# Seven half-size products for eight in w_down, for sixteen of 22 gated tiles

## The chip, the cores and the metric

One Trainium2 chip, one of its cores. The metric is the device time of one execution in microseconds (us); lower is better. In the profile PE is TensorE (matrix products), PEld its weight loads, DVE VectorE, ACT ScalarE, POOL GpSimd, SP SyncE, which issues the transfers.

## The reference

One step of a decoder layer for 1024 prompt tokens and 8 sample tokens that share the weights. The tail of the layer is what matters here:

```python
x = x + concat(ya, yb) @ w_out
x = x + cross_attn(rmsnorm(x, g_attn), mk, mv, w_q, w_o)
h = rmsnorm(x, g_ffn)
x = x + (silu(h @ w_gate) * (h @ w_up)) @ w_down     # D_MODEL 1024, D_FF 2816
y = rmsnorm(x, g_final)
```

All is float32.

## The kernel before

**Layout.** Activations lie transposed: channels on the 128 partitions, tokens along the free dimension. There are T = 1032 tokens: even prompt positions, odd ones, then the samples. The hidden dimension of 2816 is 22 tiles of 128 channels (`FF_TILES`). TH = 516 is half the tokens, TQ = 258 a quarter.

**Precision.** A float32 product is made of three passes (`PASSES`): each operand is split into a high part of TensorE's reduced type and the low rest; high x high, high x low and low x high are summed in PSUM. `split` makes the two parts: the high one on ACT or Pool, the low one (a subtraction of two SBUF operands) on DVE or Pool.

**The gated tiles.** For gate and value of a tile f the kernel already uses seven half-size products for eight (a 2 x 2 scheme of Strassen's kind): w_gate and w_up of the tile are the two column halves of one matrix, the model dimension is halved, and the tokens are halved. The operands on the token side are seven blocks `A11 ... S4`, made once and held for the whole stage in 14 of the 19 big buffers (tag `op`); those on the weight side are made tile by tile in `sums_prep` (two buffers of sums, `Ta` and `Tb`). `product` issues one of the seven: 4 blocks of channels x 3 passes x 2 quarters of 258 columns, 24 matmuls, into one two-bank PSUM buffer (two products of three) or a pair of one-bank buffers (the third). `plus` adds a product from PSUM onto a quarter of `su[f]` on DVE, `first_two`'s first product is copied by ACT, `gated` and `times_value` form silu(gate) x value on DVE, Pool and ACT. The result of tile f, 128 x 1032, goes out to the array `hd` in HBM.

**w_down.** After the 22 tiles, `down(c)` takes the hidden tiles in four chunks of four: `hidden(c)` loads each from `hd` and splits it; for each of the eight output tiles of 128 channels, 4 tiles x 3 passes x 3 thirds of 344 columns (`step3`), 36 matmuls (the profile's dn, L447), then one addition of 1032 columns onto the residual `x2` on DVE (L1409). A weight block `w_dn` of 128 x 1024 serves two output tiles: four hidden tiles by 256 outputs. The last six hidden tiles are handled by `last_down` (fd, L1435) in three spans of tokens, with the final RMSNorm of one span beside the products of the next.

**What sets the order.** Every operation is a task with costs, reads and writes (`Program.add`). `Program.order` lays the tasks out on the engines by a greedy plan: at each step the task that can start first, with a priority by program order for ties. A task with both `DVE` and `Pool` in its costs goes to whichever would end it sooner; tasks marked `lock` on DVE and all tasks on Pool are planned to exclude each other. `later` lowers the priority of preparations, and buffers come by tag from a fixed `capacity`:

```python
capacity = {"op": 19, "raw": 3, "w": 2, "scr": 3, "acc": 1, "R": 1, "sm": 4, "sst": 2, "rows": 2, "mm": 2, "ms": 2}
```

`mm` and `ms` are PSUM (three banks and one bank each). The plan is fixed when the program is built: each engine runs its tasks in that order and waits on semaphores.

Of the kernel before, what the change touches and what calls it, by code (L numbers as in the profile page):

```python
# [8 lines left out]
F32 = mybir.dt.float32  # L9
# [230 lines left out]
def hybrid_step_kernel(ctx: ExitStack, tc: tile.TileContext, io):  # L240
# [126 lines left out]

    chunks = [(0, 4), (4, 4), (8, 4), (12, 4), (16, 6)]
    last_blocks = [("w_dn", 16), ("w_dn2", 0), ("w_dn", 17), ("w_dn", 18), ("w_dn2", 1), ("w_dn", 19)]
# [12 lines left out]
    upto = len(seq)  # L382
    seq += [("w_dn", j) for j in range(16)] + last_blocks

# [875 lines left out]

    def product(w, col, b, steps=1):
# [12 lines left out]
        def emit(e, js):  # L1274
            for j in js:
                cols = slice(col + j * P, col + (j + 1) * P)
                for p, (wi, xi) in enumerate(PASSES):
                    for c in range(2):
                        e.matmul(bank(c), w[:, wi, cols], block(b, j, xi)[:, c * TQ : (c + 1) * TQ],  # L1279
                                 start=j == 0 and p == 0, stop=j == 3 and p == 2)  # L1280
# [10 lines left out]

    su = {}

# [4 lines left out]
    def plus(f, q, q2, sums):  # L1298

        a, o = part(f, q), part(f, q2)  # L1300
        from_sums(sums, "DVE", dve, lambda e, src, sl: e.tensor_tensor(as_banks(o(sl), src), src, as_banks(a(sl), src), ALU.add),  # L1301
                  [(su[f], q)], [(su[f], q2)])

# [5 lines left out]
    def gated(f, q):  # L1309
# [4 lines left out]
        times(f, q, R, RF)  # L1314

    def times_value(f, q):
        times(f, q, part(f, 2 + q), [(su[f], 2 + q)])

    def first_two(f, between=lambda: None):
        G = gu_w[f][0]  # L1320
        su[f] = op_buf(f"su{f}", (P, 4, TH))
        o = part(f, 1)
        from_sums(product(G, 0, A11, 4 if f < AHEAD else 1), "ACT", lambda n: act(n, True),
                  lambda e, src, sl: e.activation(as_banks(o(sl), src), src, AF.Copy), [], [(su[f], 1)])
        between()
        plus(f, 1, 0, product(G, 512, A12, 4 if f < AHEAD else 1))
        gated(f, 0)

    def sixth(f):
        plus(f, 1, 2, product(gu_w[f][2], 0, S2, 4 if not f else 1))  # L1330

    def others(f):
        _, U, Ta, Tb = gu_w[f]
        plus(f, 2, 3, product(Ta, 512, S3))
        fifth = product(Tb, 0, S1)
        plus(f, 2, 2, fifth)
        plus(f, 3, 1, product(Tb, 512, A22))
        plus(f, 3, 3, fifth)
        gated(f, 1)
        times_value(f, 1)  # L1340
        plus(f, 2, 2, product(U, 0, S4))
        times_value(f, 0)
        dma(lambda: hd[f], lambda: su[f][:, 0:2].rearrange("p h n -> p (h n)"), 4 * P * T, r=[(su[f], 0), (su[f], 1)], w=[("hd", f)])

    def later(work, bias="prep"):
        pg.later = BIAS[bias]
        work()
        pg.later = 0

    for n in O_ORDER:  # L1350
# [28 lines left out]

    x2 = [op_buf(f"x2_{j}") for j in range(4)]  # L1380
    hops = {c: [] for c in range(5)}

    def x2k(n):
        return [(x2[n // 2], n % 2, c) for c in range(len(LAST_SPANS))]

    state["upto"] = len(seq)
    for _ in range(2):
        w_load()

    def hidden(c):  # L1390
        for f in range(chunks[c][0], sum(chunks[c])):
            t = scr(f"ht{f}")
            dma(lambda t=t: t[:], lambda f=f: hd[f], 4 * P * T, r=[("hd", f)], w=[(t,)])
            ho = op_r(f"ho{f}")
            split(lambda p, ho=ho: ho[:, p], lambda p, ho=ho: (ho, p), lambda t=t: t[:], T, [(t,)])
            hops[c].append(ho)

    def down(c):
        for n in range(KT):
            j, i = n // 2, n % 2  # L1400
# [8 lines left out]
            add({"DVE": dve(T)}, lambda e, j=j, i=i, ps=ps: e.tensor_tensor(  # L1409
                ch3(x2[j][:, i]), ps[:, :, :CW], ch3(x2[j][:, i]), ALU.add), all3(ps) + x2k(n), x2k(n))  # L1410

    hidden(0)
    for c in range(4):
        later(lambda: hidden(c + 1))
        down(c)

# [5 lines left out]
    def last_down(c, n):  # L1422
# [8 lines left out]
        def emit(e, ks):  # L1431
            for k in ks:
                w, col = (wa, k * 256 + (n % 2) * P) if k < 4 else (wb, (k - 4) * 512 + (n % 4) * P)
                for p, (wi, xi) in enumerate(PASSES):
                    e.matmul(view(), w[:, wi, col : col + P], hops[4][k][:, xi, sl],  # L1435
                             start=(k == 0 and p == 0), stop=(k == 5 and p == 2))

        for w, keys, ks in ((wa, ka, range(4)), (wb, kb, (4, 5))):
            add({"PE": 0.000425 * 3 * len(ks) * width}, lambda e, ks=ks: emit(e, ks),
                keys + [(hops[4][k], p) for k in ks for p in range(2)], [(ps,)])  # L1440
        j, i = n // 2, n % 2
        xk = (x2[j], i, c)
        add({"DVE": dve(width)}, lambda e: e.tensor_tensor(x2[j][:, i, sl], view(), x2[j][:, i, sl], ALU.add), [(ps,), xk], [xk])
        if n < KT - 1 or c < len(LAST_SPANS) - 1:
# [139 lines left out]
```

## Time and profile before

| | us |
|---|---|
| median of 3 runs | 1268.94 (1266.14 to 1269.2) |
| the profiled execution | 1269.62, its span 1267.6 |
| granted TensorE clock, mean | 0.993 |
| gate and value products (pr), from 587.4 | 418.5 |
| w_down, tiles 0 to 15 (dn), from 1005.9 | 181.4 |
| w_down, tiles 16 to 21 (fd), from 1187.3 to the last product | 69.4 |

The times of the stages come from the chain of work that ended last, which the prediction shows with the other lines that it uses. A row of a group reads: line, engine, operation, output<-inputs by the program's names, shape, count; then busy time, mean ns of one; then the idle time of the engine just before them and what ended it. A row of the chain or the timeline starts with start and length in us. The page cuts the span into 40 slices and gives each a digit, the busy share in tenths:

```
PE   8999997999999999999999999999999999999996
DVE  7899888667367786579776766767666754312445
POOL 3578741032101102214141314232333622122100
```

PE is full from slice 18 on. The w_down stage is slices 32 to 37, where DVE's digits are lowest.

### The profile page before, as it was taken

What the parts mean: (1) busy time and instruction counts of PE and PEld (TensorE: products, weight loads), DVE (VectorE), ACT (ScalarE), POOL (GpSimd) and SP (SyncE); (2) the same over time, 40 slices, a digit from 0 to 9 for tenths busy, and PEclk for the clock granted to TensorE, in tenths of its full rate; (3) what the DMA queues carried; (4) which work ended last, traced back from release to release, by engine and by line L of the source; (5) the groups of instructions that cost most, each with busy time, mean ns of one, the idle gap of its engine ahead of it and who ended that gap; (6) DMA issues with size and microseconds to landing.
All of it is one profiled execution on the core that took longest, in us unless ns stands there. A gap on an engine that the chain in (4) does not pass through costs nothing.

```text
span 1267.6 us, 20915 instructions
## 1 busy us (share of the span) xinstructions
PE 1232.6 (97%) x8620; PEld 1212.6 (96%) x8620; DVE 844.3 (67%) x1369; ACT 476.8 (38%) x655; POOL 365.8 (29%) x304
## 2 busy tenths in 40 slices
PE   8999997999999999999999999999999999999996
PEld 7999976999999889999999999999999999999996
DVE  7899888667367786579776766767666754312445
ACT  6766648454233444453322222222222322201343
POOL 3578741032101102214141314232333622122100
PEclk9999997999999999999999999999999999999999
DMA  7447686644265673232212222121213853111112
GB/s 277 103 86 164 147 236 176 205 103 158 91 219 198 232 258 144 84 117 68 84 68 93 75 84 84 67 84 68 101 68 132 325 189 107 50 51 50 51 51 84
DMA packets 48431, 159.49 MB, mean 126 GB/s; under 512 B 7184, under 2 KB 11984, under 8 KB 47056
## 3 DMA queue, kind: packets, MB, share of 16 engines
q1 hardware_dynamic: 44736, 145.06, 32.7%
q0 software_dynamic: 3600, 13.11, 6.0%
q8 instruction: 67, 1.10, 0.4%
q14 instruction: 28, 0.23, 0.1%
HBM read 130.85 MB, written 27.30 MB: 125 GB/s over the span
## 4 chain that ended last, share of the span: by engine, by line
PE 78%; DVE 7%; issue 6%; DMA 4%; ACT 2%; POOL 2%; SPq 0%; DVEq 0%; POOLq 0%; ACTq 0%
PE pr L1279 33%; PE dn L447 14%; PE ps L447 12%; PE fd L1435 5%; PE oa L447 4%; PE ob L447 4%; DVE cacc L653 2%; DMA raw<-in_w_v 2%; PE pv L1048 2%; PE sc L990 2%; POOL w L351 1%; PE psg L447 1%; PE psv L447 1%; DMA xa<-x1d 1%; DMA w<-in_w_in 1%
## 5 line engine op out<-in xcount | busy, mean ns | idle before, releaser
L447 PE MATMUL dn<-ho,w 128*128 128x344 f32 x1152 | 181.6, 320 | 0.0
L447 PEld LDWEIGHTS dn<-ho,w 128*128 128x128 f32 x1152 | 181.4, 188 | 0.0
L1301 DVE TENSOR_TENSOR su<-pr,su 128x258 f32<-128x258 f32 (+1 forms) x204 | 108.8, 557 | 85.7 <-PE pr L1279 85.1
L1279 PE MATMUL pr<-ab,wTa 128*128 128x258 f32 x1056 | 134.2, 283 | 0.8 <-DVE su L1301 0.8
L1279 PE MATMUL pr<-ab,wG 128*128 128x258 f32 x1056 | 133.9, 283 | 0.8 <-ACT wU L340 0.8
L340 ACT ACTIVATE w<-raw 128x1024 fp32r<-128x1024 f32 (+2 forms) x54 | 52.8, 979 | 215.0 <-PE dn L447 107.6
L1279 PEld LDWEIGHTS pr<-ab,wTa 128*128 128x128 f32 x1056 | 130.1, 189 | 1.0 <-issue 1.0
L1279 PEld LDWEIGHTS pr<-ab,wG 128*128 128x128 f32 x1056 | 129.8, 189 | 1.1 <-ACT wU L340 1.1
L1279 PE MATMUL pr<-ab,wTb 128*128 128x258 f32 x1056 | 130.6, 283 | 0.0
L1279 PEld LDWEIGHTS pr<-ab,wTb 128*128 128x128 f32 x1056 | 128.6, 190 | 0.0
L351 POOL TENSOR_TENSOR w<-raw,w 128x1024 fp32r<-128x1024 f32 (+1 forms) x30 | 68.9, 2297 | 203.6 <-ACT w L340 199.3
L447 PE MATMUL ps<-xop,w 128*128 128x344 f32 x720 | 114.1, 320 | 0.7 <-DMA w<-in_w_in 0.7
L447 PEld LDWEIGHTS ps<-xop,w 128*128 128x128 f32 x720 | 113.3, 188 | 0.9 <-DMA w<-in_w_in 0.9
L1409 DVE TENSOR_TENSOR x<-dn,x 128x1032 f32<-128x1032 f32 x32 | 39.4, 1231 | 98.2 <-PE dn L447 98.2
L447 PE MATMUL ps<-xq,w 128*128 128x344 f32 x576 | 94.8, 321 | 0.0
L447 PE MATMUL po<-oo,w 128*128 128x344 f32 x576 | 91.0, 320 | 0.4 <-DVE oo L1053 0.4
L447 PEld LDWEIGHTS po<-oo,w 128*128 128x128 f32 x576 | 90.7, 188 | 0.7 <-DVE oo L1053 0.7
L447 PEld LDWEIGHTS ps<-xq,w 128*128 128x128 f32 x576 | 90.6, 188 | 0.1
L653 DVE SCALAR_TENSOR_TENSOR cacc<-glu,vec,cacc 128x511 f32<-128x511 f32 (+14 forms) x116 | 77.0, 740 | 0.0
L1435 PE MATMUL fd<-ho,w 128*128 128x388 f32 (+1 forms) x432 | 69.2, 321 | 0.0
L1435 PEld LDWEIGHTS fd<-ho,w 128*128 128x128 f32 x432 | 68.4, 188 | 0.5
L1306 DVE TENSOR_TENSOR su<-su,Rf 128x516 f32<-128x516 f32 x67 | 55.6, 832 | 18.1 <-ACT su L1313 17.4
(281 smaller groups left out, 1973.0 us busy)
## 6 DMA issues: line engine op xcount, KB each, us to landing
gr<-in_w_gu SPq DMA_DIRECT2D x44, 512.0 KB, 3.3
hd<-su SPq DMA_DIRECT2D x22, 516.0 KB, 2.9
ht<-hd SPq DMA_DIRECT2D x22, 516.0 KB, 6.2
raw<-in_w_dn SPq DMA_DIRECT2D x22, 512.0 KB, 3.3
spcache_k<-in_cache_k SPq DMA_DIRECT2D x12, 512.0 KB, 4.8
raw<-in_w_in SPq DMA_DIRECT2D x10, 512.0 KB, 5.4
w<-in_w_in POOLq DMA_DIRECT2D x9, 512.0 KB, 6.5
x<-in_xT SPq DMA_DIRECT2D x8, 516.0 KB, 6.3
```

The lines of the kernel that those rows point to most:

```text
L340: e.activation(dst(0), src(), AF.Copy, scale=1.0 if gain is None else gain)
L351: e.tensor_tensor(dst(1), src(), f32(dst(0)), ALU.subtract)
L447: e.matmul(ps[:, c, :CW], w[:, wi, cols], x[:, xi, c * CW : (c + 1) * CW], start=first and p == 0, stop=last and p == 2)
L653: e.scalar_tensor_tensor(acc[h][:, n:], src[:, : HALF - n], w, acc[h][:, n:], ALU.mult, ALU.add)
L990: e.matmul(bank()[:, i * NMEM : (i + 1) * NMEM], qop[2 * h + dt][:, qi, tt * P : (tt + 1) * P], kk[:, ki, 2 * (h % 2) + dt], start=(dt == ...
L1048: e.matmul(ps[:, c], v[:, vi, m, col : col + P], pT[h][m][:, pi, sl], start=(m == 0 and p == 0), stop=(m == 1 and p == 2))
L1279: e.matmul(bank(c), w[:, wi, cols], block(b, j, xi)[:, c * TQ : (c + 1) * TQ], start=j == 0 and p == 0, stop=j == 3 and p == 2)
L1301: from_sums(sums, "DVE", dve, lambda e, src, sl: e.tensor_tensor(as_banks(o(sl), src), src, as_banks(a(sl), src), ALU.add), [(su[f], q)], ...
L1306: add({"Pool": pool_tt(TH), "DVE": dve(TH)}, lambda e: e.tensor_tensor(o(), o(), b(), ALU.mult), r + [(su[f], q)], [(su[f], q)], lock=True)
L1409: add({"DVE": dve(T)}, lambda e, j=j, i=i, ps=ps: e.tensor_tensor(ch3(x2[j][:, i]), ps[:, :, :CW], ch3(x2[j][:, i]), ALU.add), all3(ps) + ...
L1435: e.matmul(view(), w[:, wi, col : col + P], hops[4][k][:, xi, sl], start=(k == 0 and p == 0), stop=(k == 5 and p == 2))
```

## The change

The first sixteen hidden tiles go through w_down by the same seven-for-eight scheme. A chunk of four tiles is two halves of two tiles (the inner dimension), the tokens are two halves, and 256 outputs are two halves of 128; `down(u)` does one weight block: seven products of 2 blocks x 3 passes x 2 quarters, 12 matmuls each, 16 blocks in all.

- **Token side.** The seven operand blocks of a chunk are formed where the tiles are made: of a pair of tiles (f even, then f odd) the even one's result is kept in the scratch buffer `he`, and four additions or subtractions of 516 columns (`combine`, DVE or Pool) make the sums. Blocks go out to the array `hb` in HBM in three transfers a pair (one, two and four quarters of tiles) instead of two to `hd`. `down_blocks` loads a block of 128 x 1032 and splits it: seven a chunk instead of four hidden tiles.
- **Weight side.** `dn_prep` makes four sums of 256 columns for each weight block (DVE or Pool) and splits 512, 1024 and 256 columns instead of 1024.
- **Output side.** `into` adds each product from PSUM onto a quarter on DVE, the first product of a block onto two; quarters 4 and 5 (`pp`) and quarter 3 of `x2` gather partial results, started in the first chunk by copies on ACT. In the last chunk six additions of 516 for each block (`both`, `combine`) make the outputs out of them.
- **Order.** Preparations for block u + 1 and the next chunk's blocks are added ahead of `down(u)` with lowered priority; the hidden tiles 16 to 18 are loaded ahead of the last block, 19 to 21 after it. The numbering of the seven blocks is changed so that those written together lie together.

The last six tiles, `last_down` and the final norm stay.

```diff
-A11, A12, A22, S1, S2, S3, S4 = range(7)
+A12, A22, S4, S1, A11, S2, S3 = range(7)
 O_ORDER = (0, 4, 1, 5, 2, 6, 3, 7)
 AHEAD = 2
+CHUNKS, FIRST_LAST = 4, 16
+DOWN_ORDER = (A11, S2, A12, S3, S1, A22, S4)
...
-    hd = dram.tile([FF_TILES, P, T], F32, name="hd")
+    hd = dram.tile([FF_TILES - FIRST_LAST, P, T], F32, name="hd")
+    hb = dram.tile([CHUNKS, 7, P, 2, TH], F32, name="hb")
...
+    def product(w, cols, xs, steps=1):
+        nj = len(xs[1])
         i = state["products"]
         state["products"] += 1
         if i % 3 < 2:
...
         def emit(e, js):
             for j in js:
-                cols = slice(col + j * P, col + (j + 1) * P)
                 for p, (wi, xi) in enumerate(PASSES):
                     for c in range(2):
-                        e.matmul(bank(c), w[:, wi, cols], block(b, j, xi)[:, c * TQ : (c + 1) * TQ],
-                                 start=j == 0 and p == 0, stop=j == 3 and p == 2)
-        for n in range(0, 4, 4 // steps):
-            js = range(n, n + 4 // steps)
+                        e.matmul(bank(c), w[:, wi, cols(j)], xs[0](j, xi)[:, c * TQ : (c + 1) * TQ],
+                                 start=j == 0 and p == 0, stop=j == nj - 1 and p == 2)
+        for n in range(0, nj, nj // steps):
+            js = range(n, n + nj // steps)
             add({"PE": 0.1195 * 6 * len(js)}, lambda e, js=js: emit(e, js),
-                [(w, 0), (w, 1)] + [bkey(b, j, p) for j in js for p in range(2)], [k for _, _, k in sums])
+                [(w, 0), (w, 1)] + [k for j in js for k in xs[1][j]], [k for _, _, k in sums])
         return sums
...
+    def plus_sums(o, okey, a, akey, sums):
+        from_sums(sums, "DVE", dve, lambda e, src, sl: e.tensor_tensor(as_banks(o(sl), src), src, as_banks(a(sl), src), ALU.add),
+                  [akey], [okey])
+    def copy_sums(o, okey, sums):
+        from_sums(sums, "ACT", lambda n: act(n, True), lambda e, src, sl: e.activation(as_banks(o(sl), src), src, AF.Copy), [], [okey])
+    def combine(o, okey, a, akey, b, bkey, op=ALU.add):
+        add({"Pool": pool_tt(TH), "DVE": dve(TH)}, lambda e: e.tensor_tensor(o(), a(), b(), op), [akey, bkey], [okey], lock=True)
+    su, he = {}, {}
...
+    def kept(f, q):
+        return lambda: he[f][:, q]
     def times_value(f, q):
-        times(f, q, part(f, 2 + q), [(su[f], 2 + q)])
+        if f in he:
+            combine(kept(f, q), (he[f], q), part(f, q), (su[f], q), part(f, 2 + q), (su[f], 2 + q), ALU.mult)
+        else:
+            times(f, q, part(f, 2 + q), [(su[f], 2 + q)])
+    def to_blocks(f, first, count, src, keys):
+        c, j = f // 4, f % 4 // 2
+        dma(lambda: hb[c, first : first + count, :, j].rearrange("b p t -> p b t"), src, 4 * P * TH * count, r=keys,
+            w=[("hb", c, b, j) for b in range(first, first + count)])
...
+        if f < FIRST_LAST and f % 2 == 0:
+            he[f] = scr(f"he{f}", (P, 2, TH))
+        k, e = su[f], f - 1
+        second = f < FIRST_LAST and f % 2
         times_value(f, 1)
-        plus(f, 2, 2, product(U, 0, S4))
+        if second:
+            combine(part(f, 3), (k, 3), kept(e, 1), (he[e], 1), part(f, 1), (k, 1))
+            combine(kept(e, 1), (he[e], 1), kept(e, 0), (he[e], 0), part(f, 3), (k, 3), ALU.subtract)
+            to_blocks(f, A11, 2, lambda: he[e][:], [(he[e], 0), (he[e], 1)])
+        plus(f, 2, 2, of_tokens(U, 0, S4))
         times_value(f, 0)
-        dma(lambda: hd[f], lambda: su[f][:, 0:2].rearrange("p h n -> p (h n)"), 4 * P * T, r=[(su[f], 0), (su[f], 1)], w=[("hd", f)])
+        if second:
+            combine(part(f, 2), (k, 2), part(f, 0), (k, 0), kept(e, 1), (he[e], 1))
+            to_blocks(f, A12, 4, lambda: su[f][:], [(k, q) for q in range(4)])
+        elif f in he:
+            combine(part(f, 2), (k, 2), kept(f, 0), (he[f], 0), kept(f, 1), (he[f], 1), ALU.subtract)
+            to_blocks(f, S3, 1, lambda: su[f][:, 2:3], [(k, 2)])
+        else:
+            dma(lambda: hd[f - FIRST_LAST], lambda: su[f][:, 0:2].rearrange("p h n -> p (h n)"), 4 * P * T,
+                r=[(k, 0), (k, 1)], w=[("hd", f)])
...
+    def dn_load(u):
+        dn_raw[u] = buf(f"dr{u}", "raw", (P, D))
+        dma(lambda: dn_raw[u][:], lambda: io["w_dn"][u], 4 * P * D, w=[(dn_raw[u],)])
+    def dn_prep(u):
+        raw, t = dn_raw[u], buf(f"dt{u}", "raw", (P, D))
+        W, V = buf(f"dW{u}", "w", (P, 2, 768), F32R), op_r(f"dV{u}", (P, 2, 1024))
+        dn_w[u] = W, V
+        def b(half, i):
+            return lambda: raw[:].rearrange("p (k i n) -> p k i n", k=4, i=2)[:, half::2, i]
+        def s(q):
+            return lambda: t[:].rearrange("p (q j n) -> p q j n", q=4, j=2)[:, q]
+        def minus(q, a, b, keys, op=ALU.subtract):
+            add({"Pool": pool_tt(256), "DVE": dve(256)}, lambda e: e.tensor_tensor(s(q)(), a(), b(), op), keys, [(t, q)], lock=True)
+        minus(0, b(0, 1), b(0, 0), [(raw,)])
+        minus(2, s(0), b(1, 1), [(raw,), (t, 0)])
+        minus(3, b(1, 1), b(0, 1), [(raw,)])
+        minus(1, b(1, 0), s(2), [(raw,), (t, 2)], ALU.add)
+        split(lambda p: W[:, p, :512].rearrange("p (k n) -> p k n", k=4), lambda p: (W, p, 0),
+              lambda: raw[:].rearrange("p (k i n) -> p k i n", k=4, i=2)[:, :, 0], 512, [(raw,)])
+        split(lambda p: V[:, p], lambda p: (V, p), lambda: t[:], 1024, [(t, q) for q in range(4)])
+        split(lambda p: W[:, p, 512:].rearrange("p (k n) -> p k n", k=2), lambda p: (W, p, 1), b(1, 1), 256, [(raw,)])
+    def down_blocks(c, which):
+        for b in which:
+            t = scr(f"hs{c}_{b}", (P, 2, TH))
+            dma(lambda t=t: t[:], lambda b=b: hb[c, b], 8 * P * TH, r=[("hb", c, b, j) for j in range(2)], w=[(t,)])
+            o = db[c, b] = op_r(f"hb{c}_{b}", (P, 2, 2, TH))
+            split(lambda p, o=o: o[:, :, p], lambda p, o=o: (o, p), lambda t=t: t[:], T, [(t,)])
+    def down(u):
+        c, p = u // 4, u % 4
+        W, V = dn_w.pop(u)
+        if not c:
+            dma(lambda: x2[p][:, 0], lambda: x2d[2 * p], 4 * P * T, r=[("x2d", 2 * p)], w=[q2key(p, 0), q2key(p, 1)])
+            dma(lambda: x2[p][:, 1, :TH], lambda: x2d[2 * p + 1][:, :TH], 4 * P * TH, r=[("x2d", 2 * p + 1)], w=[q2key(p, 2)])
+        def of_hidden(b, w, cols, wkeys):
+            o = db[c, b]
+            return product(w, cols, (lambda j, x: o[:, j, x], [[(o, 0), (o, 1)] + wkeys] * 2))
+        def plain(b, col):
+            part = [(W, x, 0 if col(1) < 512 else 1) for x in range(2)]
+            return of_hidden(b, W, lambda j: slice(col(j), col(j) + P), part)
+        def summed(b, q):
+            return of_hidden(b, V, lambda j: slice((2 * q + j) * P, (2 * q + j + 1) * P), [])
+        def into(q, sums, start=False):
+            if start and not c:
+                copy_sums(quarter2(p, q), q2key(p, q), sums)
+            else:
+                plus_sums(quarter2(p, q), q2key(p, q), quarter2(p, q), q2key(p, q), sums)
+        def both(q, a, b):
+            combine(quarter2(p, q), q2key(p, q), quarter2(p, a), q2key(p, a), quarter2(p, b), q2key(p, b))
+        last = c == CHUNKS - 1
+        first = plain(A11, lambda j: 2 * j * P)
+        into(3, first, True)
+        into(0, first)
+        into(3, summed(S2, 2))
+        into(0, plain(A12, lambda j: (2 * j + 1) * P))
+        into(5, summed(S3, 3), True)
+        into(4, summed(S1, 0), True)
+        into(1, summed(A22, 1))
+        if last:
+            both(4, 4, 3)
+            both(3, 3, 5)
+            both(1, 1, 3)
+            both(3, 4, 5)
+            xt = scr(f"x22_{p}", (P, TH))
+            dma(lambda: xt[:], lambda: x2d[2 * p + 1][:, TH:], 4 * P * TH, r=[("x2d", 2 * p + 1)], w=[(xt,)])
+            combine(quarter2(p, 3), q2key(p, 3), quarter2(p, 3), q2key(p, 3), lambda: xt[:], (xt,))
+        into(2, plain(S4, lambda j: 512 + j * P))
+        if last:
+            both(2, 2, 4)
+    hops = []
+    def hidden_load(f):
+        t = scr(f"ht{f}")
+        dma(lambda: t[:], lambda: hd[f - FIRST_LAST], 4 * P * T, r=[("hd", f)], w=[(t,)])
+        ho = op_r(f"ho{f}")
+        split(lambda p: ho[:, p], lambda p: (ho, p), lambda: t[:], T, [(t,)])
+        hops.append(ho)
...
+        else:
+            later(lambda: dn_load(0), "load")
+            later(lambda: dn_prep(0))
+            later(lambda: down_blocks(0, DOWN_ORDER[:4]))
...
-    def hidden(c):
-        for f in range(chunks[c][0], sum(chunks[c])):
-            t = scr(f"ht{f}")
-            dma(lambda t=t: t[:], lambda f=f: hd[f], 4 * P * T, r=[("hd", f)], w=[(t,)])
-            ho = op_r(f"ho{f}")
-            split(lambda p, ho=ho: ho[:, p], lambda p, ho=ho: (ho, p), lambda t=t: t[:], T, [(t,)])
-            hops[c].append(ho)
-    def down(c):
-        for n in range(KT):
-            j, i = n // 2, n % 2
-            if i == 0:
-                state["wd"] = w_take("w_dn")
-            w, wkeys = state["wd"]
-            ps = mm_buf(f"dn{c}_{n}")
-            for k in range(4):
-                step3(ps, w, wkeys, out_cols(i)(k), hops[c][k], k, k == 0, k == 3)
-            if not c:
-                dma(lambda j=j, i=i: x2[j][:, i], lambda n=n: x2d[n], 4 * P * T, r=[("x2d", n)], w=x2k(n))
-            add({"DVE": dve(T)}, lambda e, j=j, i=i, ps=ps: e.tensor_tensor(
-                ch3(x2[j][:, i]), ps[:, :, :CW], ch3(x2[j][:, i]), ALU.add), all3(ps) + x2k(n), x2k(n))
-    hidden(0)
-    for c in range(4):
-        later(lambda: hidden(c + 1))
-        down(c)
+    later(lambda: down_blocks(0, DOWN_ORDER[4:]))
+    units = 4 * CHUNKS
+    for u in range(units):
+        c, p = u // 4, u % 4
+        if u + 1 < units:
+            later(lambda: dn_load(u + 1), "load")
+            later(lambda: dn_prep(u + 1))
+        if c + 1 < CHUNKS and p >= 1:
+            later(lambda: down_blocks(c + 1, ((), DOWN_ORDER[:2], DOWN_ORDER[2:4], DOWN_ORDER[4:])[p]))
+        if u == units - 1:
+            state["upto"] = len(seq)
+            for _ in range(2):
+                later(w_load, "load")
+        if u == units - 2:
+            for f in range(FIRST_LAST, FIRST_LAST + 3):
+                later(lambda: hidden_load(f))
+        down(u)
+    for f in range(FIRST_LAST + 3, FF_TILES):
+        hidden_load(f)
```

More of the change, by code (lines that the diff above doesn't have):

```diff
@@ L382, in hybrid_step_kernel @@
     upto = len(seq)
-    seq += [("w_dn", j) for j in range(16)] + last_blocks
+    seq += last_blocks
     state = {"taken": 0, "loaded": 0, "prepped": 0, "upto": upto}
@@ L1290, in from_sums, with of_tokens @@
             add({engine: cost(sl.stop - sl.start)}, lambda e, src=src, sl=sl: emit(e, src(), sl), [key] + r, w)
-    su = {}
+    def plus_sums(o, okey, a, akey, sums):
[6 more added lines that the diff above has]
+    su, he = {}, {}
+    def of_tokens(w, col, b, steps=1):
+        return product(w, lambda j: slice(col + j * P, col + (j + 1) * P),
+                       (lambda j, p: block(b, j, p), [[bkey(b, j, p) for p in range(2)] for j in range(4)]), steps)
     def part(f, q):
@@ L1298, in plus @@
     def plus(f, q, q2, sums):
-        a, o = part(f, q), part(f, q2)
-        from_sums(sums, "DVE", dve, lambda e, src, sl: e.tensor_tensor(as_banks(o(sl), src), src, as_banks(a(sl), src), ALU.add),
-                  [(su[f], q)], [(su[f], q2)])
+        plus_sums(part(f, q2), (su[f], q2), part(f, q), (su[f], q), sums)
     def times(f, q, b, r):
@@ L1321, in first_two @@
         su[f] = op_buf(f"su{f}", (P, 4, TH))
-        o = part(f, 1)
-        from_sums(product(G, 0, A11, 4 if f < AHEAD else 1), "ACT", lambda n: act(n, True),
-                  lambda e, src, sl: e.activation(as_banks(o(sl), src), src, AF.Copy), [], [(su[f], 1)])
+        copy_sums(part(f, 1), (su[f], 1), of_tokens(G, 0, A11, 4 if f < AHEAD else 1))
         between()
-        plus(f, 1, 0, product(G, 512, A12, 4 if f < AHEAD else 1))
+        plus(f, 1, 0, of_tokens(G, 512, A12, 4 if f < AHEAD else 1))
@@ L1327, in first_two @@
         gated(f, 0)
     def sixth(f):
[L1330 removed]
+        plus(f, 1, 2, of_tokens(gu_w[f][2], 0, S2, 4 if not f else 1))
     def others(f):
         _, U, Ta, Tb = gu_w[f]
[L1334 to L1335 removed]
+        plus(f, 2, 3, of_tokens(Ta, 512, S3))
+        fifth = of_tokens(Tb, 0, S1)
         plus(f, 2, 2, fifth)
[L1337 removed]
+        plus(f, 3, 1, of_tokens(Tb, 512, A22))
@@ L1348, in later, with quarter2, q2key @@
         pg.later = 0
+    x2 = [op_buf(f"x2_{j}") for j in range(4)]
+    pp = [op_buf(f"pp{j}", (P, 4, TH)) for j in range(2)]
+    dn_raw, dn_w, db = {}, {}, {}
+    def quarter2(p, q):
+        if q < 4:
+            return lambda sl=slice(0, TH): x2[p][:].rearrange("p i (h t) -> p (i h) t", h=2)[:, q, sl]
+        return lambda sl=slice(0, TH): pp[p // 2][:, p % 2 * 2 + q - 4, sl]
+    def q2key(p, q):
+        return (x2[p], "q", q) if q < 4 else (pp[p // 2], p % 2 * 2 + q - 4)
+    def dn_load(u):
+        dn_raw[u] = buf(f"dr{u}", "raw", (P, D))
+        dma(lambda: dn_raw[u][:], lambda: io["w_dn"][u], 4 * P * D, w=[(dn_raw[u],)])
@@ L1439, in last_down @@
             add({"PE": 0.000425 * 3 * len(ks) * width}, lambda e, ks=ks: emit(e, ks),
-                keys + [(hops[4][k], p) for k in ks for p in range(2)], [(ps,)])
+                keys + [(hops[k], p) for k in ks for p in range(2)], [(ps,)])
         j, i = n // 2, n % 2
         xk = (x2[j], i, c)
-        add({"DVE": dve(width)}, lambda e: e.tensor_tensor(x2[j][:, i, sl], view(), x2[j][:, i, sl], ALU.add), [(ps,), xk], [xk])
+        add({"DVE": dve(width)}, lambda e: e.tensor_tensor(x2[j][:, i, sl], view(), x2[j][:, i, sl], ALU.add),
+            [(ps,), xk, q2key(j, 2 * i), q2key(j, 2 * i + 1)], [xk])
         if n < KT - 1 or c < len(LAST_SPANS) - 1:
```

11 lines of the change are left out of this document (1 added, 10 removed).

## The prediction

> **What bounds the kernel now.** I read the page first, then the chain of work that ended last in order of time, then the waits of TensorE, and last the windows and groups of the stage that the change rewrites.
>
> ```profile
> PE 1232.6 (97%) x8620; PEld 1212.6 (96%) x8620; DVE 844.3 (67%) x1369; ACT 476.8 (38%) x655; POOL 365.8 (29%) x304
> PE pr L1279 33%; PE dn L447 14%; PE ps L447 12%; PE fd L1435 5%; PE oa L447 4%; PE ob L447 4%; DVE cacc L653 2%; DMA raw<-in_w_v 2%; PE pv L1048 2%; PE sc L990 2%; POOL w L351 1%; PE psg L447 1%; PE psv L447 1%; DMA xa<-x1d 1%; DMA w<-in_w_in 1%
> ...
> 587.40 418.52 PE pr L1279 x3480
> 1005.92 181.42 PE dn L447 x1152
> 1187.34 28.73 PE fd L1435 x162
> ...
> 1243.19 13.54 PE fd L1435 x114
> ...
> PE pr L1279 <- DVE su L1301: 0.8, 1, 0.8
> ```
>
> The second line is the chain's share by line; the four after it are the chain in order of time (start, length, work); the last is the whole list of TensorE's waits between 587 and 1187 us. From 587 us on the end is set by matmuls alone: 418.5 us of gate and value products (pr), 181.4 us of w_down for the first sixteen tiles (dn), then w_down of the last six (fd). TensorE waited once, 0.8 us, in 600 us. So whatever shortens dn on TensorE shortens the run, as long as TensorE stays fed.
>
> **TensorE's own time.** The spacing of matmuls comes from the chain: 418.52 / 3480 = 120.3 ns for 258 columns (pr), 181.42 / 1152 = 157.5 ns for 344 (dn), 28.73 / 162 = 177.3 ns for 388 (fd). The first two give 0.433 ns a column and 8.6 ns fixed; that line puts 388 columns at 176.6, near the third, and fd runs in groups of 12 and 6 matmuls. So I take no extra for short groups. After the change one unit (512 hidden channels into 256 outputs) is 7 products x 2 blocks x 3 passes x 2 halves = 84 matmuls of 258 columns, and 16 units are 1344: 1344 x 120.3 = 161.6 us for 181.4. **TensorE: -19.8 us.** The columns are exactly 7/8, and the fixed part of the 192 more matmuls takes back under 2 us.
>
> [...]
>
> **What is added on DVE, Pool and ACT.** Columns of the next rows: operation and shape with its count, then busy us and mean ns of one. The timeline rows give start, length, engine.
>
> ```profile
> L1301 DVE TENSOR_TENSOR su<-pr,su 128x516 f32<-128x516 f32 x104 | 71.7, 691 | 73.4 <-PE pr L1279 73.1
> L1301 DVE TENSOR_TENSOR su<-pr,su 128x258 f32<-128x258 f32 x100 | 37.7, 418 | 12.2 <-PE pr L1279 12.0
> L1443 DVE TENSOR_TENSOR x<-fd,x 128x256 f32<-128x256 f32 x8 | 3.3, 420 | 2.5 <-PE fd L1435 2.3
> L1409 DVE TENSOR_TENSOR x<-dn,x 128x1032 f32<-128x1032 f32 x32 | 39.4, 1231 | 98.2 <-PE dn L447 98.2
> L351 DVE TENSOR_TENSOR wTa<-ta,wTa 128x1024 fp32r<-128x1024 f32 x16 | 20.0, 1249 | 1.1 <-ACT wTa L340 1.1
> L351 POOL TENSOR_TENSOR wTa<-ta,wTa 128x1024 fp32r<-128x1024 f32 x6 | 14.5, 2409 | 0.0
> L1306 DVE TENSOR_TENSOR su<-su,Rf 128x516 f32<-128x516 f32 x67 | 55.6, 832 | 18.1 <-ACT su L1313 17.4
> L1306 POOL TENSOR_TENSOR su<-su 128x516 f32<-128x516 f32 x6 | 7.8, 1304 | 8.9 <-DVE su L1306 8.9
> ...
> 802.00 1.22 DVE L351 TENSOR_TENSOR wTa<-ta,wTa 128x1024 fp32r<-128x1024 f32 x1
> 803.13 0.69 DVE L1306 TENSOR_TENSOR su<-su,Rf 128x516 f32<-128x516 f32 x1
> ...
> 819.71 0.69 DVE L1239 TENSOR_TENSOR tb<-gr,gr 128x512 f32<-128x512 f32 x1 [0.20 <-DMA gr<-in_w_gu]
> 820.32 0.68 DVE L1239 TENSOR_TENSOR ta<-gr 128x512 f32<-128x512 f32 x1
> 820.92 0.68 DVE L1239 TENSOR_TENSOR ta<-tb,gr 128x512 f32<-128x512 f32 x1
> ...
> 700.00:800.00 100.00, 100.00 (x834) 100.00 (x833) 69.09 (x100) 24.01 (x33) 32.24 (x21) 1.00 0.23 80
> 1006.00:1187.00 181.00, 181.00 (x1151) 181.00 (x1150) 69.09 (x54) 36.44 (x35) 41.72 (x18) 1.00 0.31 106
> ```
>
> The last two rows are windows (length, then busy time of PE, PEld, DVE, ACT, POOL). Consecutive DVE operations start 0.61 us apart though each lasts 0.68, and 1.13 apart for 1.22: back to back an operation costs some 0.08 us less than its length. So 0.61 for 516 wide, 0.34 for 256 or 258, 1.13 for 1024; Pool needs 1304 / 691 or 2409 / 1249, about 1.9 times as long as DVE.
>
> In the gated stage each pair of the first sixteen tiles gets four additions of 516 more: 2.4 us on DVE per 40.4 us, or 6 in 100, where DVE idles 31 in 100 and Pool 68. Price nothing: DVE goes to 75%; were that cover gone, 8 x 2.4 = 19 us. ACT gets nothing there. The SP queue issues three transfers a pair for two; behind them wait only loads of gate and value weights, at a DMA share of 0.23.
>
> In the w_down stage a unit of 10.1 us (84 x 120.3 ns) now asks of DVE: eight evacuations of 516 (seven products, the first added twice), a third of them as two halves: 8 x (2/3 x 0.61 + 1/3 x 0.68) = 5.1 us, where before two of 1.23 served 11.3 us. Only DVE (and ACT, for three of the eight in the first chunk) can do these. Then work that DVE or Pool may do: four sums of weights, 4 x 0.34 = 1.4; low parts of 1024, 512 and 256, 1.13 + 0.61 + 0.34 = 2.1; low parts of the hidden blocks, 7 of 1032 for four units, 1.75 x 1.14 = 2.0. Together 5.4, and 10.5 with the evacuations: more than the 10.1 us that DVE has, so Pool must help. If Pool and DVE exclude each other on this work (next rows), moving y of the 5.4 to Pool needs 10.5 - y <= L on DVE and 5.4 + 0.9 y <= L for the pair; they meet at y = 2.7, L = 7.8: 78% of the unit. In the last chunk (40.4 us) the block splits fall away; six additions of 516 a unit come in (4 x 3.7), and the splits of three hidden tiles and two weights (5 x 1.13), beside three units' weights (3 x 3.5) and evacuations of 20.3 us. By the same sums L is 40.4, all of it, or 36.7 (91%) if the last unit's additions slip into fd, whose results alone need them.
>
> ```profile
> 990.24 1.23 DVE L351 TENSOR_TENSOR ho<-ht,ho 128x1032 fp32r<-128x1032 f32 x1 [0.92 <-ACT ho L340]
> 990.32 3.44 POOL L351 TENSOR_TENSOR ho<-ht,ho 128x1032 fp32r<-128x1032 f32 x1
> ...
> 991.54 0.69 DVE L1301 TENSOR_TENSOR su<-pr,su 128x516 f32<-128x516 f32 x1
> ...
> 992.15 2.70 DVE L351 TENSOR_TENSOR ho<-ht,ho 128x1032 fp32r<-128x1032 f32 x1
> ```
>
> Pool's 2.4 us operation took 3.44 beside DVE's 1.23, then DVE's took 2.70 until Pool was done; the evacuation between them, with one input in PSUM, kept its 0.69. So evacuations pass, sums and splits don't, and what queues behind a blocked split on DVE, an evacuation, waits with it.
>
> **The added wait.** Three products fit the PSUM rotation. Before, a dn product took 36 x 157.5 ns = 5.7 us and two fitted, so DVE had 5.7 us to empty one. Now a product takes 1.44 us and has two others behind it: 2.9 us, less the 0.7 of the evacuation, 1.4 for the doubled one. A single 1.13 split ahead of an evacuation does no harm; two, or one blocked like the 2.70 above, hold TensorE up by some 0.4 us. No row shows the stage at 78% load. From below the bound is zero, the pr stage (0.8 us in 419; a gain is excluded, as TensorE is already gapless). From above, taking lengths for intervals, it is the DVE rival below. I take 0.4 us for each of the first 12 units, 0.8 for each of the last 4, nearer to the pr stage, whose products have the same form: 4.8 + 3.2 = **+8 us**.
>
> Sum: 1269.6 (the profiled execution, span 1267.6) - 19.8 + 8 = 1257.8. The median of the runs is 0.7 lower, so **1257 us**, a saving of 12. A change of 0.3% (3.8 us) is about what can be told from none here.
>
> **Rivals.**
> *TensorE is simply fed* (stalls under 3 us): 1250. For it: pr at 69% DVE with no stall. Against it: half the PSUM time, more load.
> *DVE becomes the bound.* For it: taken with their lengths, the operations of a unit are 8 x (2/3 x 0.69 + 1/3 x 0.84) = 5.9 and 4 x 0.42 + 1.25 + 0.69 + 0.42 + 1.75 x 1.25 = 6.2, 12.1 for 10.1 us. If Pool takes only the quarter that it takes of low parts now (6 of 22 wTa above), DVE keeps 5.9 + 4.7 = 10.6, and with waits at the port, as in the 832 ns that 691 become (20% of 4.7), 11.5; a unit of the last chunk comes to 13.7, and the first chunk, with its copies on ACT, isn't bound. Over: 1.4 x 8 + 3.6 x 4 = 26 us, so 1275. It decides from 19.8 / 16 = 1.24 us lost per unit. Against it: the intervals, and that in the pr stage, where lengths would put DVE at its limit too, it sat idle for TensorE for 73.4 us. Three quarters of it, about 1268, would be no change.
> *The seam into fd starves.* Three of its six hidden tiles are asked for only after the last unit; landing takes 6.2 us and the splits 2.3. Cover: freed slots early in the last unit, 10 us before. If it fails, up to 6 us: 1263.
>
> ```profile
> ht<-hd SPq DMA_DIRECT2D x22, 516.0 KB, 6.2
> ```
>
> *The smaller matmuls cost more than the line says.* At 135 ns (181.4 / 1344) nothing is gained; with stalls, slower at 1277 or so. The 120.3 of 3480 like ones speaks against it. *The change does not do what it says* (no fewer columns) is excluded by the count.
>
> **Chances.** Forecast (stalls 3 to 15 us, 1252 to 1264) 0.53; simply fed 0.16; seam 0.05; half-bound, no change, 0.08; DVE-bound 0.16; dearer matmuls 0.02. Faster by over 0.3%: 0.53 + 0.16 + 0.05 = 0.74; same 0.08; slower 0.18. The range runs from no stall at all, 1248, to most of the DVE-bound case, 1273; what is left out is under 2 in 10.
>
> **What would show it.** Right: 1344 matmuls of 258 columns near 120 ns in this stage, some 170 us long; the list of TensorE's waits naming DVE's evacuations, 5 to 12 us in all, most in the last chunk; pr still about 418 us. Wrong: DVE over 95% busy through the stage with waits of 20 us or more (DVE-bound); spacing over 125 ns with no waits named (matmuls); waits in pr on weights or in fd on hidden tiles.

## The result and the profile after

The changed kernel takes 1269.97 us (median of 14 runs, 1267.44 to 1273.04); the kernel before, on the same chip, 1269.12. The ratio is 1.0007, 95% interval 0.9994 to 1.0019: no change. The forecast was 1257. The profiled execution of the changed kernel took 1273.0, the slowest of the fourteen; 2.2 us of that were lost ahead of the gated stage, whose first product starts at 559.9 us, before at 557.7.

The chain of work that ended last, from the end of the gated tiles on (start, length, work), shows where the gain went. It is the changed kernel's.

```profile
589.55 407.04 PE pr L1283 x3384
997.87 7.83 DMA hs<-hb
1005.79 1.08 ACT hb L344
1006.89 2.23 DVE hb L355
1009.12 0.68 DVE su L1298 x2
...
1016.65 130.33 PE pr L1283 x1080
1152.65 4.58 PE pr L1283 x36
...
1163.24 7.52 PE pr L1283 x48
...
1173.11 8.40 DVE x L1306 x3
1181.51 1.22 DVE x L1298 x2
1182.86 7.96 PE pr L1283 x48
1190.82 28.67 PE fd L1570 x162
```

Before, one row covered this stage: 181.42 us of gapless matmuls. Now 1080 matmuls stand in one row, 130.33 / 1080 = 120.7 ns each, where a line of 120.3 was expected; at both ends of it TensorE waits. From the last product of tile 21 (1008.1) to the first of fd (1190.7) are 182.6 us, for 181.3 before. TensorE's waits between 587 and 1191 us, all of them, and windows of the changed kernel (PE, PEld, DVE, ACT, POOL busy, granted clock, DMA share, GB/s):

```profile
PE pr L1283 <- DVE x L1298: 13.7, 4, 7.8
PE pr L1283 <- DVE su L1298: 3.4, 2, 2.6
...
1018.00:1138.00 120.00, 120.00 (x999) 119.90 (x999) 96.71 (x159) 48.81 (x69) 84.82 (x63) 1.00 0.47 148
1138.00:1191.00 53.00, 40.72 (x305) 40.17 (x304) 42.85 (x59) 11.37 (x14) 30.61 (x20) 0.87 0.36 120
1163.20:1170.80 7.60, 7.55 (x50) 7.58 (x51) 3.94 (x9) 0.00 (x0) 3.28 (x3) 0.78 0.52 176
1182.80:1190.80 8.00, 7.94 (x49) 7.97 (x50) 3.94 (x8) 2.12 (x2) 0.01 (x1) 0.72 0.67 258
```

Of the 17.1 us of waits 0.8 was there before. The other 16.3: 4.0 at the start of the stage (2.6 and 1.4), 12.3 in the last chunk (1.35, 3.15 and 7.8). For 120 us between, with DVE 81% and Pool 71% busy, TensorE did not wait at all. After the two longer pauses the granted clock was 0.78 and 0.72, and 48 matmuls took 7.52 and 7.96 us, 157 and 166 ns each: with the 36 at 127 that makes 4 us more. So -19.8 + 16.3 + 4 = +0.5. The stage grew 1.3; 0.5 of the rest is the 0.4 ns by which a matmul was dearer than the line, times 1344. The gated stage was not touched: 448.2 us from its first to its last matmul in both traces.

The 7.8 us pause in the timeline of the changed kernel, Pool's rows first, then DVE's, then TensorE's:

```profile
1172.06 6.13 POOL L355 TENSOR_TENSOR w<-raw,w 128x1024 fp32r<-128x1024 f32 x2
1178.15 2.81 POOL L355 TENSOR_TENSOR ho<-ht,ho 128x1032 fp32r<-128x1032 f32 x1
...
1170.79 0.70 DVE L1298 TENSOR_TENSOR x<-pr,x 128x516 f32<-128x516 f32 x1 [0.79 <-PE pr L1283]
1171.40 1.79 DVE L355 TENSOR_TENSOR ho<-ht,ho 128x1032 fp32r<-128x1032 f32 x1
1173.11 2.87 DVE L1306 TENSOR_TENSOR x<-pp 128x516 f32<-128x516 f32 x1
1175.91 2.84 DVE L1306 TENSOR_TENSOR x<-x,pp 128x516 f32<-128x516 f32 x1
1178.67 2.84 DVE L1306 TENSOR_TENSOR x<-x,x 128x516 f32<-128x516 f32 x1
1181.43 2.55 DVE L1298 TENSOR_TENSOR x<-pr,x 128x516 f32<-128x516 f32 x5
...
1173.47 1.61 PE L1283 MATMUL pr<-hb,dW 128*128 128x258 f32 x12
1182.86 6.52 PE L1283 MATMUL pr<-hb,dV 128*128 128x258 f32 x36 [7.78 <-DVE x L1298]
```

TensorE has finished three products by 1175.1 and then waits until DVE has emptied one of their PSUM buffers. DVE has three final additions (L1306) ahead of the five evacuations in its order. Each is an operation of 0.68 (as at 1160.54, with nothing on Pool), and each takes 2.85 here, beside Pool's splits: it ends 0.55 us after one of them has ended (at 1175.43, 1178.19 and 1180.96). The prediction's rows at 990 to 995 us show the like: a split on Pool took 3.44 beside DVE's of 1.23, then DVE's next took 2.70. The prediction and the first expectation call this waits at a port; what makes the two engines wait for each other, no trace shows. The evacuations wait behind the additions until 1181.4.

### The profile page after: what moved, and what is told of

Its sections match the earlier page's. It is cut to its first block, busy times and chain, and to the rows that moved or that the text cites. A ratio compares the mean times of both kernels' runs of the same rounds, so it can differ in the third digit from the quotient of the medians.

```text
span 1270.9 us, 21766 instructions
## 1 busy us (share of the span) xinstructions
PE 1218.7 (96%) x8812; PEld 1196.9 (94%) x8812; DVE 951.6 (75%) x1579; ACT 514.5 (40%) x718; POOL 449.3 (35%) x377
## 4 chain that ended last, share of the span: by engine, by line
PE 83%; DVE 9%; DMA 3%; ACT 2%; issue 2%; SPq 0%; POOL 0%; DVEq 0%; ACTq 0%; POOLq 0%
PE pr L1283 46%; PE ps L450 13%; PE po L450 7%; PE fd L1570 5%; PE oa L450 4%; PE ob L450 4%; DVE cacc L656 2%; PE sc L993 2%; PE pv L1051 2%; DMA raw<-in_w_v 1%; DVE x L1306 1%; DMA hs<-hb 1%; DMA w<-in_w_in 1%; DMA xraw<-in_xT 1%; PE pt L1032 0%
## 5 line engine op out<-in xcount | busy, mean ns | idle before, releaser
L1283 PE MATMUL pr<-hb,dV 128*128 128x258 f32 x768 | 101.7, 290 | 13.7 <-DVE x L1298 13.7
L1283 PEld LDWEIGHTS pr<-hb,dV 128*128 128x128 f32 x768 | 98.1, 196 | 14.5 <-issue 12.8
L1298 DVE TENSOR_TENSOR x<-pr,x 128x516 f32<-128x516 f32 (+1 forms) x122 | 63.2, 554 | 20.4 <-PE pr L1283 19.5
L1283 PE MATMUL pr<-hb,dW 128*128 128x258 f32 x576 | 74.7, 283 | 2.6 <-DVE su L1298 2.6
L344 ACT ACTIVATE w<-raw 128x1024 fp32r<-128x1024 f32 (+2 forms) x37 | 34.5, 941 | 100.1 <-issue 37.6
L1283 PEld LDWEIGHTS pr<-hb,dW 128*128 128x128 f32 x576 | 71.6, 189 | 2.7 <-ACT dW L344 2.7
```

The costliest lines, as they stand in the source:

```text
L344: e.activation(dst(0), src(), AF.Copy, scale=1.0 if gain is None else gain)
L1283: e.matmul(bank(c), w[:, wi, cols(j)], xs[0](j, xi)[:, c * TQ : (c + 1) * TQ], start=j == 0 and p == 0, stop=j == nj - 1 and p == 2)
```

## The experiments

Theory A: what counts is the order on DVE. Additions and splits with two SBUF inputs, lengthened while Pool runs its own, stand ahead of evacuations. Theory B: DVE and Pool have too much work in the last chunk. Theory C: three short products are too little PSUM. Ratios are to the kernel before, run on the same chip (medians 1268.1 to 1268.3).

**Additions left out.**

```diff
-        last = c == CHUNKS - 1
+        last = False
```

> The six additions of 516 columns that each weight block of the last chunk makes at the end are left out (24 in all, with the four loads of a residual quarter), so the output is not the layer's. In the changed kernel TensorE idled 17 us between the gated tiles and the last six: 4.3 at the start of the w_down stage, 13 in its last chunk, and the matmuls after the pauses were slower by about 4 us. Theory A (additions on DVE stand behind Pool's splits at the shared port, and PSUM evacuations stand behind the additions in DVE's order): the 13 us and the 4 us go, 4.3 stay; about 1252. Theory B (DVE and Pool simply have too much work in the last chunk): the same here, about 1252. Theory C (a PSUM rotation of three short products is too shallow): the pauses stay, about 1268.

1258.0 us, ratio 0.992 (0.990 to 0.993), where A and B had both said 1252. C falls. The 7.8 us pause is gone, and one of 3.2 has stayed, so the additions aren't alone: splits ahead of evacuations do it too. A pair of splits that takes 1.01 us in the changed kernel (1161.48) took 5.47 here beside two on Pool, and three evacuations stood behind it:

```profile
PE pr L1283 <- DVE x L1298: 4.6, 2, 3.2
...
1150.58 5.26 POOL L355 TENSOR_TENSOR ho<-ht,ho 128x1032 fp32r<-128x1032 f32 x2
1150.65 5.47 DVE L355 TENSOR_TENSOR dW<-dr,dW 128x512 fp32r<-128x512 f32 x2
1156.05 1.89 DVE L1298 TENSOR_TENSOR x<-pr,x 128x516 f32<-128x516 f32 x3
```

**All low parts of the last chunk on DVE.** `split` gets a switch `pin` that leaves the low part one engine:

```diff
+            if pin["lo"]:
+                lo = {pin["lo"]: lo[pin["lo"]]}
...
+        pin["lo"] = "DVE" if u > 4 * (CHUNKS - 1) else None   # dn_prep; the same around hidden_load and last_w
```

> From the last chunk on (weight blocks 13 to 15, hidden tiles 16 to 21, the weights of the last six tiles) all low parts are made on DVE, none on Pool; all else as in the changed kernel. Work moves from Pool (eight operations of 2.4 to 3.1 us in that stretch) to DVE. Theory A: nothing of 2.4 us stands on Pool any more, an addition waits 1.3 us at most, the pauses of the last chunk fall from 13 us to 3 or less and the slow matmuls with them; about 1258. Theory B: DVE, 81% busy there with its waits, gets some 9 us more, the pauses grow; 1272 or more. Theory C: as the changed kernel, 1270.

1258.9 us, ratio 0.993 (0.992 to 0.995). DVE got more work and the kernel got 11 us faster. From 1136.8 us to the last six tiles DVE was busy 40.8 of 44.0 us, 93%, where the changed kernel has 42.7 of 52.7, 81%, from 1138: B falls for DVE; Pool, which the edit relieves, had been busy 58% of that stretch in the changed kernel. The waits in the trace are 9.6 us instead of 17.1, none over 2.2; 5.3 of them are in the last chunk, for 12.3 before the edit and 3 or less expected. The profiled execution was the slowest of the four, 1262.6.

```profile
PE pr L1287 <- DVE x L1302: 6.0, 4, 2.2
PE pr L1287 <- DVE su L1302: 2.9, 2, 2.1
PE pr L1287 <- DVE pp L1302: 0.7, 1, 0.7
```

What is left of it is order alone, with nothing on Pool. At 1157.97 DVE began two additions and three splits in a row, at 0.68 and 0.69 us an addition and 0.69, 1.22 and 0.42 the splits, with an evacuation behind them:

```profile
1157.97 0.68 DVE L1310 TENSOR_TENSOR x<-x,pp 128x516 f32<-128x516 f32 x1
1158.58 0.69 DVE L1310 TENSOR_TENSOR x<-x,x 128x516 f32<-128x516 f32 x1
1159.18 0.69 DVE L359 TENSOR_TENSOR dW<-dr,dW 128x512 fp32r<-128x512 f32 x1
1159.78 1.22 DVE L359 TENSOR_TENSOR dV<-dt,dV 128x1024 fp32r<-128x1024 f32 x1
1160.92 0.42 DVE L359 TENSOR_TENSOR dW<-dr,dW 128x256 fp32r<-128x256 f32 x1
1161.25 1.29 DVE L1302 TENSOR_TENSOR x<-pr,x 128x516 f32<-128x516 f32 x2
1162.09 4.63 PE L1287 MATMUL pr<-hb,dV 128*128 128x258 f32 x24 [1.88 <-DVE x L1302]
```

**Only the last weights' low parts on DVE.** The same switch, around `last_w` alone:

> Of the changed kernel one thing is altered: the low parts of the weights of the last six tiles, two of which stood on Pool (2.4 us each) where TensorE paused for 8 us, are made on DVE alone. Theory A (an addition on DVE that meets a split on Pool waits for all of it, and the evacuations behind it wait too): the 8 us pause falls to 3 or less, the two earlier pauses of the last chunk (1.5 and 3.3 us) stay, since other splits are still on Pool; at fd up to 3.6 us may be waited for late splits; 1264. Theory B (too much work for DVE): DVE gets 2.3 us more in that unit, the pause stays at 8 us or grows; 1270 or more.

1265.2 us, ratio 0.997 (0.996 to 0.999). 1264 was expected. This is the narrowest test of what Pool's splits do to DVE's additions. DVE's order is the same at that place, Pool's splits are gone from it, and the three additions take 0.68 each; the pause is 1.3 us instead of 7.8. A wait of 2.4 for a weight appears at the seam into the last six tiles.

```profile
1170.69 0.68 DVE L1310 TENSOR_TENSOR x<-pp 128x516 f32<-128x516 f32 x1
1171.29 0.68 DVE L1310 TENSOR_TENSOR x<-x,pp 128x516 f32<-128x516 f32 x1
1171.90 0.68 DVE L1310 TENSOR_TENSOR x<-x,x 128x516 f32<-128x516 f32 x1
1172.51 2.55 DVE L1302 TENSOR_TENSOR x<-pr,x 128x516 f32<-128x516 f32 x5
```

**Additions on Pool alone.**

```diff
-            combine(quarter2(p, q), ..., quarter2(p, b), q2key(p, b))
+            combine(quarter2(p, q), ..., quarter2(p, b), q2key(p, b), on=("Pool",))   # the same for the residual quarter
```

> The additions of the last chunk go to Pool alone (1.3 us each for 0.69); DVE keeps evacuations and splits. Theory A: no addition stands ahead of an evacuation, TensorE's waits on evacuations inside the last chunk fall to 3 us or less; Pool with 7.8 us of additions per 10 us of a weight block is late with the splits for the last six tiles, which may cost up to 6 us at that seam; about 1260. Theory B: Pool is over its limit and holds back weights, pauses of 13 us or more stay, now with weight splits named; 1270 or more.

1262.9 us, ratio 0.996 (0.994 to 0.997). The last chunk has no wait left; the stage up to fd is 166.8 us instead of 182.6. But with Pool full of additions a hidden tile's low part on DVE is late, TensorE waits 4.1 us at the seam, and the matmuls behind it run at a granted clock of 0.76 on the mean (window 1176 to 1190). A part of the gain is lost in another place.

```profile
PE fd L1570 <- DVE ho L355: 4.1, 1, 4.1
...
1176.00:1190.00 14.00, 9.50 (x41) 9.23 (x42) 14.00 (x8) 5.63 (x6) 12.48 (x6) 0.76 0.50 165
```

**The additions last in the program.** The same additions, on the same two engines:

```diff
-        if last:
-            both(4, 4, 3)                  # and the other five, in down(u)
+    def finish(p):
+        both(4, 4, 3)                      # and the other five
...
     last_w = {block: w_take(block[0]) for block in last_blocks}
+    for p in range(4):
+        finish(p)
```

> The same six additions for each weight block of the last chunk, on DVE or Pool as before, but added to the program after the last weight block, so that the plan ranks them behind every evacuation and split; nothing is taken away. Theory A (what counts is what stands ahead of an evacuation in DVE's order, not how much work there is): the pauses of the last chunk fall from 13 us to 4, as where the additions were left out, and the additions run beside the last six tiles, where DVE has room; 1259. Theory B (too much work for DVE and Pool): the work is all still there, it must be done before the outputs of the last six tiles are added; 8 us or more of pauses in the chunk or at the seam; 1266 or more.

1258.1 us, ratio 0.992 (0.990 to 0.994): as much as without the additions, with all of the work done. Most of it is done later: 15 of the 24 additions start after the last six tiles' first product (1180.0), and from 1136.7 us to there DVE is busy 35.1 us. So this run takes load out of the last chunk as well as delays out of DVE's order, and does not tell A from B by itself; low_on_dve and last_weights_on_dve do. The waits of the stage are 7.3 us, 4.1 of them in the last chunk, as A had said:

```profile
PE pr L1283 <- DVE x L1298: 3.2, 1, 3.2
PE pr L1283 <- DVE su L1298: 3.2, 2, 2.4
PE pr L1283 <- DVE pp L1298: 0.9, 1, 0.9
```

**The start of the stage.** In the chain above the pause of 2.6 us leads back to a hidden block (hs<-hb) that landed 7.8 us after its issue; its low part on DVE, waiting for it and then 2.23 us long beside one on Pool (1.22 alone, at 996.52), stood ahead of tile 21's evacuations. Three edits aimed at it. First, the low parts of the first chunk's blocks on Pool alone:

> The low parts of the first chunk's seven hidden blocks are made on Pool alone (in the changed kernel four of them were on DVE, one waiting for a late load with evacuations behind it). Theory A: the pause of 2.7 us at the end of the gated tiles goes, that of 1.6 us after the first product may stay; the last chunk is as in the changed kernel; 1267. Theory B: Pool gets 5 us more before the first product, the pause at this seam grows by that; 1274.

1269.8 us, ratio 1.001 (0.999 to 1.003), a miss. The first pause went, as expected, but one of 2.0 us came some ten microseconds later, and the waits of the stage came to 14.6 us for 16.3.

Next, both moves of the last chunk together (additions on Pool, low parts on DVE, four hidden tiles ahead of the last block), without and with an edit at the start:

> Both moves together: in the last chunk the additions are on Pool alone and the low parts on DVE alone; and four of the last six hidden tiles are asked for ahead of the last weight block, not three. Theory A: no 2.4 us operation on Pool, no addition ahead of an evacuation: pauses inside the last chunk 2 us or less, at the seam into the last six tiles 2 us or less, the 4.3 us at the start of the stage stay; 1268.5 - 19.8 + 4.3 + 3 = 1256. Theory B: each engine has its own overload (Pool 7.8 of 10 us, DVE 9 of 10): pauses of 8 us or more; 1261 or more.

> As roles, and the loads of the residual for the first chunk's additions are planned after each block's weights instead of as early as possible, so that they do not share the transfers with the first hidden blocks. If the pauses at the start of the stage come from a hidden block that lands late behind those loads (its low part stands on DVE ahead of evacuations): 4.3 us fall to 1 or less; 1252. If they come from DVE's load at that seam: as roles.

> As roles, and the first of the first chunk's hidden blocks is loaded and split a tile earlier (beside tile 20's successor's weights instead of tile 21's products). If a late hidden block is what DVE waits for at the start of the stage: the pause of 2.7 us goes, that of 1.6 may stay; 1253. If DVE's load at that seam is the cause: 0.5 us better than roles at most.

```diff
-        dma(..., r=[("x2d", 2 * p)], ...)                   # roles_late_residual: both residual loads
+        dma(..., r=[("x2d", 2 * p), (V, 0)], ...)
...
+            if f == FF_TILES - 2:                           # roles_early_block
+                later(lambda: down_blocks(0, DOWN_ORDER[:1]))
```

1266.0 (0.998; 0.996 to 1.000), 1268.0 (0.999; 0.998 to 1.001) and 1263.2 us (0.995; 0.994 to 0.997). Roles is a miss by 10 us. Its profiled execution took 1262 and its twelve runs lie between 1262 and 1272. The spread goes with the granted clock of the run: 0.990 to 0.995 in the four under 1264, 0.986 to 0.989 in the other eight (the last section comes back to it). Its trace shows that separate roles don't keep DVE's operations from getting longer: two splits that take 1.2 each alone took 4.56 us beside Pool's additions, and TensorE paused 3.0 us behind them.

```profile
1161.20 2.21 POOL L1310 TENSOR_TENSOR pp<-pp,x 128x516 f32<-128x516 f32 x1 [2.91 <-DVE pp L1302]
1162.17 4.56 DVE L359 TENSOR_TENSOR ho<-ht,ho 128x1032 fp32r<-128x1032 f32 x2
1163.49 2.15 POOL L1310 TENSOR_TENSOR x<-x,pp 128x516 f32<-128x516 f32 x1
1166.66 2.55 DVE L1302 TENSOR_TENSOR x<-pr,x 128x258 f32<-128x258 f32 x5
1167.72 1.71 PE L1287 MATMUL pr<-hb,dW 128*128 128x258 f32 x12 [3.00 <-DVE x L1302]
```

The later residual loads did not help: the pause at the start stayed, and two more came in the first chunk. That the transfers shared with the residual make the block late is not shown. The earlier block did take the first pause away.

**The best of it.** Last, the early block with each of the two edits that worked, and with both (there all six hidden tiles are also asked for ahead of the last block):

> low_on_dve (its pauses: 4 us at the start of the stage, 6 in the last chunk) with the first hidden block a tile earlier: the start loses 1 to 3 us; 1257.

> As adds_last, and the first of the first chunk's hidden blocks a tile earlier. In roles this took 1 to 3 us off the start of the stage; 1257 by theory A, 1264 or more by theory B.

> As adds_last_early, the low parts of the last chunk on DVE alone, and all six last hidden tiles asked for ahead of the last weight block. Theory A: no split of 2.4 us on Pool, additions last: pauses of the last chunk 1 us, at the seam into the last six tiles 3 us or less; 1254. Theory B: DVE, with the low parts and the evacuations, falls behind; 1262 or more.

1257.9 us (0.992; 0.990 to 0.993), 1257.4 (0.991; 0.989 to 0.993) and 1257.9 (0.991; 0.990 to 0.993). The three can't be told apart from each other or from adds_last, and the last is some 4 us short of the 1254 expected. Any of them is 0.8 or 0.9% below the kernel before. With both edits the waits of the stage fall to some 4 us, but 3.3 us for a weight at the seam take their place.

## Why the prediction was wrong

**TensorE's own time: right.** 1344 matmuls, at 120.7 ns where nothing waits (1080 in one row), for the 120.3 of the line. **The gated stage at no cost: right**, to 0.1 us in 448.

**The load: about right on DVE.** L was worked out as 7.8 us of a 10.1 us unit, 78%; DVE was busy 81% of the 120 us in the middle, with its lengthening beside Pool counted as busy (its four splits of 256 columns took 1.14 us each there, 0.41 alone). Pool was busy 71%, where the same sum gives 2.7 x 1.9 = 5.1 of 10.1, half.

**The stall term: the step that failed.** It was "0.4 us for each of the first 12 units, 0.8 for each of the last 4", 8 us. The first part, 4.8 us, is near the 4.0 that were waited at the start of the stage, but by luck: away from that seam none of these units paused. The last part, 3.2 us, was four times too low: 12.3 us. Its working allowed for one blocked split; it did not ask what stands in a row on DVE when six additions a unit, planned at 0.61 each, meet Pool's splits. Three of them made 8.4 us. Its own load sum had found 36.7 to 40.4 of 40.4 us in the last chunk, and the term was still taken "nearer to the pr stage". Two things were not asked about at all: the start of the stage (only the seam into fd was feared), and the clock after a pause, some 4 us of slow matmuls.

**The rival that came true** is the half-bound case, no change, 0.08, in its time but not in its mechanism. That rival was a matter of DVE's load, and low_on_dve, which adds to it, is faster. The row of a split lengthened beside Pool, 2.70 us for 1.23, stood in the prediction; what that costs was taken as a share of load instead of as a delay for everything queued behind. The 1257 of the sum is about what the same work takes once the order is mended (1257.4 to 1258.9), with waits in other places than the sum had them.

**What the plan has to do with it.** `Program.order` plans DVE's locked tasks and Pool's not to overlap, but only in planned time; no semaphore keeps them apart. In the gated stage, with products twice as long behind each evacuation, that was harmless (0.8 us of waits). That is argued from the code; the slip of the real order against the planned one was not measured.

## What to carry to other kernels

When a change shortens the bound engine's work and puts more on the engine that feeds it, don't stop at the load: list what stands ahead of each feeding operation in that engine's order, take each at the length it has when it is blocked, and compare the sum with the slack of the buffer. Work that nobody needs soon (here the final additions) belongs last in the order, even where it is short. A pause on TensorE can cost more than its length: here the granted clock was 0.50 for 3.41 us after the one of 3.15, and the 36 matmuls from 1163.24 took 6.06 us, for 4.59 of the 36 from 1016.65 at 1.00.

## What was not expected of the hardware

**The granted clock after a pause.** In the changed kernel (windows as above):

```profile
1159.97:1163.38 3.41, 0.26 (x3) 0.17 (x2) 3.41 (x7) 1.06 (x1) 0.69 (x2) 1.00 0.26 74
1163.38:1166.79 3.41, 3.41 (x17) 3.41 (x18) 1.68 (x4) 0.00 (x0) 1.79 (x1) 0.50 0.84 270
...
1173.62:1177.03 3.41, 1.46 (x13) 1.25 (x11) 3.41 (x2) 0.07 (x1) 3.41 (x2) 1.00 0.56 155
1177.03:1187.27 10.24, 4.41 (x20) 4.44 (x21) 7.65 (x8) 3.00 (x3) 3.93 (x2) 0.50 0.47 169
```

From the end of the gated tiles to 1205 us the granted clock was 0.50 in these two stretches, 3.41 and 10.24 us long, which begin 13.65 us apart, and 1.00 elsewhere; the 0.78 and 0.72 above are means over a half part and a full part. In the 3.41 us ahead of them TensorE was idle for 3.15 and 1.95 us. In the 3.41 us from 1006.37, from 1013.19 and from 1149.73 (each a whole number of such lengths ahead of the first row) it was idle for 1.67, 1.36 and 1.35, and the clock after them stayed at 1.00.

The length of a pause alone does not tell its cost. In roles TensorE paused 1.92 and 3.00 us between 1140 and 1180 us, where the granted clock was 1.00, and the 36 and 12 matmuls behind took 4.57 and 1.71 us. In low_on_dve the 24 matmuls behind a pause of 1.88 us took 4.63 us (24 from 1166.55 took 3.05), and the 12 behind one of 2.16 took 1.68; the granted clock from 1140 to 1180 was 0.96 on the mean. That the idle time within such a window decides is the author's estimate from the five figures of the changed kernel; that such differences make the whole spread of roles is not shown.

**DVE's additions beside Pool's queue.** Three splits stood in a row on Pool in the changed kernel, of 3.37, 2.80 and 2.81 us (2.41 for the one from 1157.65), and three additions on DVE took 2.87, 2.84 and 2.84 us for 0.68. Each addition ended 0.55 us after one of the splits, the first two before the next split had ended; no addition waited for all three.
